# A two-layer attention and retention trunk: bias rows written two rounds later, the output weights' squares started a stage earlier, and the output projection's loads issued in written order

## The chip, the cores and the metric

The kernel runs on one core of a Trainium2 chip. The metric is the device time of one execution in microseconds (us); lower is better. TensorE (PE) multiplies, ScalarE (ACT), VectorE (DVE) and GpSimd (POOL) work on what it produces, and SyncE (SP) issues every DMA of this kernel from one queue, in order.

## The reference

```python
def chunked_rel_attention(q, k, v, rel_bias):      # 8 heads of 64, chunks of 64, own chunk and 8 before
    scores = einsum("bnqhd,bnkhd->bnhqk", qc, kb) * dh ** -0.5
    bias = rel_bias[:, clip(dist, -REL_CLIP, REL_CLIP) + REL_CLIP]
    p = softmax(where(valid, scores + bias, NEG_INF))
    return einsum("bnhqk,bnkhd->bnqhd", p, vb)

def hybrid_layer(x, norm_gain, w_in, w_out, rel_bias, cos, sin):
    proj = rms_norm(x, norm_gain) @ w_in           # x (1, 2048, 1024), w_in (1024, 4096)
    aq, ak, av, ag, rq, rk, rv, rg = split(proj)   # eight sections of 512
    ya = chunked_rel_attention(aq, ak, av, rel_bias)
    yr = chunkwise_retention(rq, rk, rv, cos, sin) # 4 heads of 128, a state from chunk to chunk
    y = concatenate([ya * silu(ag), yr * silu(rg)])
    return x + y @ w_out                           # w_out (1024, 1024)

def reference(x, ...):
    for layer in range(2):
        x = hybrid_layer(x, ...)
    return rms_norm(x, final_gain)
```

## The kernel before

**Split products.** Every large product is float32 made of three float16 products: a tensor is kept as a high and a low half (`hTh`/`hTl`, `whT`/`wlT`, `whV`/`wlV`, `whO`/`wlO`), and a dense tile is 24 matmuls of 128x128 by 128x512 (8 slices of the inner dimension by 3 products), in thirds of 8.

**Stages.** A layer has four groups `s` (two attention heads and one retention head each), and a group four quarters `n` of 512 rows. For each (layer, group, quarter) there are two stages of twelve rounds, a round being 8 matmuls. `dense_T` makes the four feature-major tiles (attention q and k, retention q and k; `dT` in the trace). `dense_V` makes four token-major tiles (values and gates; `dV`). Beside them, a round each time, runs the attention and retention of the quarter *before* (`attention`, `retention`): eight units of three rounds, one for each row tile `a` and head `hx`. A name such as pT1_0_3_0_0 holds layer, group, quarter, row tile and head.

**A unit.** PE makes the scores `S`; DVE adds the bias and takes the maximum (`sc`, L819); ACT takes the exponential (L822) and the high half `pq` (L824); POOL subtracts for the low half (L825); a transposing DMA turns both into `pT` (L827); two units after the scores PE multiplies `pT` by the values (`o`, L835 to L837). Retention multiplies `r` (L869) from `dT` (written by ACT L873 and DVE L877) and the state's halves `sh`. The dense tiles have two PSUM buffers (`psD`): a tile can start when the tile two before it has been read out, for `dense_V` by ACT L775 to L778 and last by DVE L781 to L785 (`gt`).

**Order.** PE, ACT, DVE and POOL execute in the order in which the code is written. `later(k, ...)` puts work k rounds on, `push(generator, steps)` hands background work (weights for the next group) to a list of which `run` takes a share in every round. On SP a list scheduler orders the DMAs, except that those marked by `in_turn` or `keep_in_program_order` may not be moved ahead of what is written before them. A DMA that waits for its buffer holds all DMAs behind it on SP.

**What is touched.** `bias_scratch` writes, at the first quarter of a group, two heads' bias rows 128 times each into HBM (`toep`, L567, 128x767), and `bias_tiles` reads them back skewed (`bias`, L580), masks two corners on POOL and scales on ACT. `prep_Omax` reads `w_out` in eight loads of 512 KB (`stO0m0` to `stO0m7` in layer 0) and squares them on ACT (L312) to find one scale; it is pushed in the second stage of (group 2, quarter 2), and it has the three buffers of the pool `w4`. `prep_O` makes the halves of `w_out`. `wout_first` prepares the first two row tiles of the finished `y` (`yyy`): squares (L963), scale, high rows (L226), low rows (L232); `y_turn` transposes them to `yhy`/`yly`. `wout` is the output projection: sixteen steps of 48 matmuls (`dO`, L1110), six rounds each, with row loads of `y` (`y_load`, L945) and `x` (`x_load`, L954), the sum into `x` (DVE L1113), the store `x_d` (L1119), and in layer 0 the next layer's norm (`residual`: L1006, transposes `ptn` L1011 on PE for some tiles). In its first four steps it runs beside the last attention.

Of the kernel before, what the change touches and what calls it, by code (L numbers as in the profile page):

```python
# [18 lines left out]
P = 128  # L19
# [8 lines left out]
def hybrid_trunk(ctx: ExitStack, tc: tile.TileContext, x, pos, gain, gcol, w_in, w_out, rel, fgain,  # L28
# [468 lines left out]
    def prep_Omax(l, go):  # L497
        nm = f"O{l}"
        mm = b2.tile([P, 1], F32, tag="omax", name=f"omax{nm}")
        st = load_sec(w_out[l, :, 0:P], f"{nm}m0")  # L500
        for j in range(KT):
            yield
            m1 = sumsq(st, f"{nm}m{j}", None)
            if j + 1 < KT:
                st = load_sec(w_out[l, :, (j + 1) * P:(j + 2) * P], f"{nm}m{j + 1}")
            if j == 0:
                dve.tensor_copy(mm, m1)
            else:
# [428 lines left out]
    def y_load(l, t):  # L937
        u = St()
        u.nm = f"y{l}_{t}"
        u.t = t  # L940
        if t < 8:
            u.y = w4.tile([P, D], F32, tag="w4", name=f"yy{u.nm}")
        else:
            u.y = b2.tile([P, D], F32, tag="q", name=f"yy{u.nm}")
        sp.dma_start(u.y, y_d[t])  # L945
        return u

    def x_load(l, u):
# [3 lines left out]
        else:  # L952
            u.x = w4.tile([P, D], F32, tag="w4", name=f"xx{u.nm}")
        sp.dma_start(u.x, x[u.t * P:(u.t + 1) * P, :] if l == 0 else x_d[u.t])  # L954

# [102 lines left out]
    def wout_first(l, go, us):  # L1058
# [4 lines left out]
        for fns in ((), (lambda: y_squares(l, u),), (lambda: y_scale(u, go),), (lambda: rows_hi(u.rows, u.y, u.sy),),  # L1063
                    (lambda: rows_lo(u.rows, u.y, u.sy), lambda: y_squares(l, v)), (lambda: y_turn(u), lambda: y_scale(v, go)),
                    (lambda: rows_hi(v.rows, v.y, v.sy),), (lambda: rows_lo(v.rows, v.y, v.sy),)):
            yield
            for fn in fns:
                fn()
        yield

    def wout(l, go, gc, us, wT=None):
# [6 lines left out]
        for r in range(6 * NT):  # L1078
# [10 lines left out]
            if (i == 1 and T + 1 < NT and (end or T + 2 < NT)) or (i == 5 and hurry):  # L1089
                y_turn(us[T + 1 if i == 1 else T + 2])  # L1090
            if i == 0 and T + 2 < NT:
                us.append(y_load(l, T + 2))
            if i == 1 and T + 1 < NT:
# [282 lines left out]
    for l in range(DEPTH):  # L1376
        gO = [Grp(), Grp()]
        go = Grp()
        for s in range(NSW):
            g = grp(l, s)  # L1380
            for n in range(NS):
# [7 lines left out]
                if n == 0 and not first:  # L1389
                    bs, bt = bias_scratch(l, s), bias_tiles(l, s, g)  # L1390
                    later(1, lambda bs=bs: next(bs))
                    for k in (6, 10, 17, 21):
                        later(k, lambda bt=bt: next(bt))
# [18 lines left out]
                if n == NS - 1 and s == 1 and l + 1 < DEPTH:  # L1412
                    gain_load(l + 1)
                if not first:
                    run(dT, att, 10 if n == 0 else 14 if (l, s, n) == (0, 0, NS - 1) else 22 if (l, s) == (0, 0) else 24)
                if n == NS - 1 and s == NSW - 1:
                    us = []
                    push(wout_first(l, go, us), 10)
                if n == 2 and s == 2:
                    push(prep_Omax(l, go), 13)  # L1420
                if n == NS - 1:
                    if s + 1 < NSW:
                        push(prep_V(l, s + 1, grp(l, s + 1)), 23)
                    else:
                        push(prep_O(l, 1, gO[1], go), 9)
                run(dense_V(l, s, n, g, st), att, 24 if n == NS - 1 and s < NSW - 1 else 12)
# [90 lines left out]
```

## Time and profile before

| | |
|---|---|
| Runs | median of 3: 2081.31 us (2080.66 to 2084.2) |
| Profiled execution | 2082.83 us; its span, first to last instruction, 2081.1 us |
| Mean granted TensorE clock | 0.991 |
| Busy | PE 2006.5 us (96%), DVE 1229.8 (59%), ACT 1139.5 (55%), POOL 683.5 (33%) |
| DMA | 313.63 MB, 65.5% of 16 engines |

Busy time of PE counts pipelined matmuls as covered, so the span less PE's busy time (74.6 us) is what PE stood still. A table of windows gives for stretches of the span their length, each engine's busy time, the mean granted clock (PEclk) and the busy share of the DMA engines: length less PE's busy time is that stretch's standstill, and a clock under 1.00 is time lost at half rate. A row of waits reads: waiting instruction <- releaser: us in total, times, longest. In a timeline a row is start, duration, engine, line, operation, with the idle time before it and its releaser in brackets; SPq rows are the issue of a DMA and not its transfer.

### The profile page before, as it was taken

The numbers are of one execution on the slowest core, as the hardware profiler recorded it, in microseconds if no ns is written. First come the engines' busy times: TensorE is split into PE (matmuls) and PEld (weight loads), VectorE is DVE, ScalarE is ACT, GpSimd is POOL, SyncE is SP. The second block draws the span as 40 slices with busy tenths as digits, with TensorE's granted clock in tenths as the row PEclk, the third lists the DMA queues.
The fourth block names the chain that finished last, engine by engine and source line by source line (L and its number), as shares of the span: only waits on it lengthen the run. The fifth ranks groups of instructions, "written<-read, shape, count | busy, mean of one in ns | idle before, by whom it ended". The sixth has DMA issues, their size and how long they took to land.

```text
span 2081.1 us, 39317 instructions
## 1 busy us (share of the span) xinstructions
PE 2006.5 (96%) x14014; PEld 1052.0 (51%) x14014; DVE 1229.8 (59%) x3817; ACT 1139.5 (55%) x2530; POOL 683.5 (33%) x701
## 2 busy tenths in 40 slices
PE   6988999999999999998999999999999999999998
PEld 4444545555555555544444555555555555554543
DVE  7776556566556555576653556555655565557643
ACT  7566665556565644555443546554655565446432
POOL 0244343444334434430002333444334334343100
PEclk9999999999999999999999999999999999999999
DMA  8678674547484854799765546554755776548874
GB/s 237 162 153 180 142 148 112 114 110 164 117 182 113 167 137 102 153 234 260 203 163 118 125 104 148 120 126 103 152 111 128 178 146 161 127 102 192 211 199 125
DMA packets 645701, 313.63 MB, mean 151 GB/s; under 512 B 459232, under 2 KB 602080, under 8 KB 645504
## 3 DMA queue, kind: packets, MB, share of 16 engines
q1 hardware_dynamic: 645504, 311.12, 65.5%
q8 instruction: 109, 1.79, 0.4%
q14 instruction: 88, 0.72, 0.1%
HBM read 123.26 MB, written 41.98 MB: 79 GB/s over the span
## 4 chain that ended last, share of the span: by engine, by line
PE 49%; DMA 2%; ACT 2%; DVE 1%; issue 0%; SPq 0%; POOL 0%; POOLq 0%; ACTq 0%; DVEq 0%
PE dT L748 15%; PE dV L767 14%; PE dO L1110 13%; PE r L869 2%; DMA pT<-pq 1%; PE S L816 1%; PE S L815 1%; PE o L835 1%; PE o L836 1%; PE o L837 1%; ACT stO1m L312 0%; ACT sc L822 0%; PE ptn L1011 0%; DVE sc L819 0%; ACT pq L824 0%
## 5 line engine op out<-in xcount | busy, mean ns | idle before, releaser
L825 POOL TENSOR_TENSOR pq<-sc,pq 128x640 f16<-128x640 f32 (+4 forms) x256 | 319.6, 1248 | 872.1 <-ACT pq L824 460.2
L822 ACT ACTIVATE sc<-sc,mq,cT 128x640 f32<-128x640 f32 (+4 forms) x256 | 218.4, 853 | 629.4 <-DVE rl L841 338.3
L767 PE MATMUL dV<-whV,hTh 128*128 128x512 f16 x1024 | 353.1, 381 | 4.3 <-DVE gt L785 4.2
L767 PE MATMUL dV<-wlV,hTh 128*128 128x512 f16 x1024 | 353.2, 381 | 0.0
L767 PE MATMUL dV<-whV,hTl 128*128 128x512 f16 x1024 | 353.1, 380 | 0.0
L748 PE MATMUL dT<-hTh,whT 128*128 128x512 f16 x1008 | 349.2, 382 | 2.1 <-DMA hTh<-xa 1.1
L748 PE MATMUL dT<-hTh,wlT 128*128 128x512 f16 x1008 | 348.0, 380 | 0.0
L748 PE MATMUL dT<-hTl,whT 128*128 128x512 f16 x1008 | 347.8, 380 | 0.0
L767 PEld LDWEIGHTS <-hTh 128*128 128x128 f16 x2048 | 196.8, 98 | 219.2 <-DVE gt L785 6.5
L748 PEld LDWEIGHTS <-whT 128*128 128x128 f16 x2016 | 193.0, 98 | 214.9 <-issue 10.6
L819 DVE CUSTOM_DVE_ANT_0 sc<-S,bias 128x640 f32<-128x640 f32 (+4 forms) x256 | 188.3, 736 | 112.7 <-PE S L816 111.3
L1110 PE MATMUL dO<-whO,yly 128*128 128x512 f16 x512 | 194.6, 380 | 1.5 <-DMA yly<-hTl 0.8
L1110 PE MATMUL dO<-whO,yhy 128*128 128x512 f16 x512 | 194.8, 381 | 1.0 <-DMA yhy<-hTh 1.0
L1110 PE MATMUL dO<-wlO,yhy 128*128 128x512 f16 x512 | 194.8, 380 | 0.0
L824 ACT ACTIVATE pq<-sc 128x640 f16<-128x640 f32 (+4 forms) x256 | 171.5, 670 | 8.1
L1110 PEld LDWEIGHTS <-yhy 128*128 128x128 f16 x1024 | 99.9, 98 | 116.1 <-DMA yhy<-hTh 1.5
L767 PEld LDWEIGHTS <-hTl 128*128 128x128 f16 x1024 | 99.3, 98 | 110.6 <-issue 1.9
L748 PEld LDWEIGHTS <-wlT 128*128 128x128 f16 x1008 | 97.5, 98 | 113.1 <-issue 6.2
L815 PE MATMUL S<-k,q 128*128 128x128 f16 (+3 forms) x592 | 142.9, 268 | 0.2
L835 PE MATMUL o<-v,pT 128*128 128x65 f16 x1120 | 130.0, 194 | 12.3 <-DMA pT<-pq 12.3
L836 PE MATMUL o<-v,pT 128*128 128x64 f16 x1120 | 130.2, 195 | 0.0
L816 PE MATMUL S<-k,q 128*128 128x128 f16 (+3 forms) x592 | 130.2, 268 | 0.0
(352 smaller groups left out, 3462.1 us busy)
## 6 DMA issues: line engine op xcount, KB each, us to landing
q<-qq SPq DMA_DIRECT2D x128, 128.0 KB, 2.4
yyy<-y_d SPq DMA_DIRECT2D x32, 512.0 KB, 4.7
stT<-in_w_in_dram SPq DMA_DIRECT2D x27, 512.0 KB, 5.1
stV<-in_w_in_dram SPq DMA_DIRECT2D x26, 512.0 KB, 4.7
k<-kk SPq DMA_DIRECT2D x128, 64.0 KB, 2.0
swp<-rot SPq DMA_DIRECT2D x64, 128.0 KB, 2.7
tabc<-tab SPq DMA_DIRECT2D x32, 256.0 KB, 3.0
tabs<-tab SPq DMA_DIRECT2D x32, 256.0 KB, 3.2
```

The lines of the kernel that those rows point to most:

```text
L748: pe.matmul(ps, w_[:, j, kt, :], h_[:, kt, :], start=(m == 0), stop=(m == 23))
L767: pe.matmul(ps, h_[:, kt, a * P:(a + 1) * P], w_[:, kt, :], start=(m == 0), stop=(m == 23))
L815: pe.matmul(o, st.q[:, hx, 0, cs], k_, start=True, stop=False)
L816: pe.matmul(o, st.q[:, hx, 1, cs], k_, start=False, stop=True)
L819: dve.tensor_tensor_reduce(out=v, in0=S[:, 0:w], in1=g.bias[hx][:, 640 - w:640], scale=1.0, scalar=-3.0e38, op0=ALU.add, op1=ALU.max, accu ...
L822: act.activation(v, v, AF.Exp, bias=m[:, 0:1], scale=g.c[:, 0:1])
L824: act.activation(pq[:, 0:w], v, AF.Copy)
L825: pool.tensor_tensor(pq[:, w:2 * w], v, pq[:, 0:w], op=ALU.subtract)
L835: pe.matmul(o[:, 0:65], u.p[:, b, :], v_[:, 0:65], start=(b == 0), stop=False)
L836: pe.matmul(o[:, 0:64], u.p[:, b, :], v_[:, 65:129], start=False, stop=False)
L869: pe.matmul(out_, w_, m_, start=(i == 0), stop=(i + 1 == len(pairs)))
L1110: pe.matmul(ps, h_[:, kt, :], w_[:, kt, :], start=(m == 0), stop=(m == 23))
```

## The change

Five edits. (1) The writing of the bias rows is put off from one round into the group to three, and reading them back by one round. (2) `prep_Omax` is pushed one stage earlier, spread over 21 steps, and keeps two loads in flight ahead of the squares. (3) `wout_first` is pushed one stage earlier too, `y_turn` of the first tile stands at a fixed round of the last stage, and `prep_O` of the second half has that stage to itself. (4) `y` rows are loaded half a step earlier than before by the code (in round 3 of the step before). (5) `y` loads from row tile 2 on and `x` loads from row tile 1 on are held to the written order on SP.

```diff
     def prep_Omax(l, go):
         nm = f"O{l}"
         mm = b2.tile([P, 1], F32, tag="omax", name=f"omax{nm}")
-        st = load_sec(w_out[l, :, 0:P], f"{nm}m0")
+        load = lambda j: load_sec(w_out[l, :, j * P:(j + 1) * P], f"{nm}m{j}")
+        for _ in range(4):
+            yield
+        sts = [load(0), load(1)]
+        for _ in range(4):
+            yield
         for j in range(KT):
             yield
-            m1 = sumsq(st, f"{nm}m{j}", None)
-            if j + 1 < KT:
-                st = load_sec(w_out[l, :, (j + 1) * P:(j + 2) * P], f"{nm}m{j + 1}")
+            m1 = sumsq(sts[j], f"{nm}m{j}", None)
+            if j + 2 < KT:
+                sts.append(load(j + 2))
@@ y_load
-        sp.dma_start(u.y, y_d[t])
+        i = sp.dma_start(u.y, y_d[t])
+        if t > 1:
+            in_turn(i)
@@ x_load
-        sp.dma_start(u.x, x[u.t * P:(u.t + 1) * P, :] if l == 0 else x_d[u.t])
+        i = sp.dma_start(u.x, x[u.t * P:(u.t + 1) * P, :] if l == 0 else x_d[u.t])
+        if u.t:
+            in_turn(i)
@@ wout_first
-                    (..., lambda: y_squares(l, v)), (lambda: y_turn(u), lambda: y_scale(v, go)),
+                    (..., lambda: y_squares(l, v)), (lambda: y_scale(v, go),),
...
+    def with_turn(gen, us):
+        for r in range(12):
+            if r == 7:
+                y_turn(us[0])
+            next(gen, None)
+            yield
@@ wout
-            if i == 0 and T + 2 < NT:
-                us.append(y_load(l, T + 2))
+            if r == 0 or (i == 3 and T + 3 < NT):
+                us.append(y_load(l, T + 3 if r else 2))
@@ the loop over the stages
-                    later(1, lambda bs=bs: next(bs))
-                    for k in (6, 10, 17, 21):
+                    later(3, lambda bs=bs: next(bs))
+                    for k in (7, 11, 17, 21):
                         later(k, lambda bt=bt: next(bt))
...
+                if n == 2 and s == 2:
+                    push(prep_Omax(l, go), 21)
+                last = n == NS - 1 and s == NSW - 1
+                if last:
+                    us = []
+                    push(wout_first(l, go, us), 9)
                 if not first:
-                    run(dT, att, 10 if n == 0 else ... else 24)
-                if n == NS - 1 and s == NSW - 1:
-                    us = []
-                    push(wout_first(l, go, us), 10)
-                if n == 2 and s == 2:
-                    push(prep_Omax(l, go), 13)
+                    run(dT, att, 12 if last else 10 if n == 0 else ... else 24)
                 if n == NS - 1:
...
-                        push(prep_O(l, 1, gO[1], go), 9)
+                        push(with_turn(prep_O(l, 1, gO[1], go), us), 12)
                 run(dense_V(l, s, n, g, st), att, 24 if n == NS - 1 and s < NSW - 1 else 12)
```

No instruction is added or removed: PE, ACT, DVE, POOL and SP issue the same work in another order. Three places show it.

SP at the start of group 1 of layer 1, before (`stT` is a 512 KB load of the next group's weights, `q1_1_0` the copies of q):

```order
L850 DMA y_d10_115<-ya1_0_2_2_0_16319 128x128
L567 DMA toep1_2_16466<-rel_d_141 128x767
L567 DMA toep1_3_16468<-rel_d_141 128x767
L297 DMA stT1_20_17262<-in_w_in_dram 128x8x128
L827 DMA_TRANSPOSE pT1_0_3_0_0_16499<-pq1_0_3_0_0_16496 128x10x128
L657 DMA q1_1_0_16535<-qq1_1_0_16536 64x1024 x4
```

The same place now:

```order
L855 DMA y_d10_115<-ya1_0_2_2_0_16319 128x128
L297 DMA stT1_20_17262<-in_w_in_dram 128x8x128
L832 DMA_TRANSPOSE pT1_0_3_0_0_16495<-pq1_0_3_0_0_16492 128x10x128
L572 DMA toep1_2_16537<-rel_d_141 128x767
L572 DMA toep1_3_16539<-rel_d_141 128x767
L662 DMA q1_1_0_16531<-qq1_1_0_16532 64x1024 x4
```

The two bias writes have moved from ahead of the transpose to behind it; ten rows on, the read `bias1_2` has moved from ahead of the copies of k to just ahead of the transpose pT1_0_3_1_0. Of the six groups that follow another in a layer, five change in this way. In the first (layer 0, group 1) the scheduler puts the two writes *earlier* than before, between the weight load `stV0_13` and the transpose pT0_0_2_3_1, and not behind a transpose.

ACT where `dense_T` of layer 1, group 2, quarter 2 ends and `dense_V` begins, before:

```order
L824 ACTIVATE pq1_2_1_1_1_21110<-sc1_2_1_1_1_21105 128x640
L917 ACTIVATE state1_2_0_20299<-state1_2_0_20299 128x128
L681 ACTIVATE raw1_2_2_21141<-dT1_2_2_3_21070 128x512
L822 ACTIVATE sc1_2_1_2_0_21191<-sc1_2_1_2_0_21191,mq1_2_1_2_0_21192,cT1_2_17591 128x640
L824 ACTIVATE pq1_2_1_2_0_21196<-sc1_2_1_2_0_21191 128x640
L312 ACTIVATE stO1m0_21206,m1O1m0_21208<-stO1m0_21206 128x1024
```

The same place now:

```order
L829 ACTIVATE pq1_2_1_1_1_21115<-sc1_2_1_1_1_21110 128x640
L312 ACTIVATE stO1m0_20959,m1O1m0_21119<-stO1m0_20959 128x1024
L922 ACTIVATE state1_2_0_20299<-state1_2_0_20299 128x128
L312 ACTIVATE stO1m1_20961,m1O1m1_21142<-stO1m1_20961 128x1024
L686 ACTIVATE raw1_2_2_21156<-dT1_2_2_3_21075 128x512
L312 ACTIVATE stO1m2_21121,m1O1m2_21171<-stO1m2_21121 128x1024
L827 ACTIVATE sc1_2_1_2_0_21211<-sc1_2_1_2_0_21211,mq1_2_1_2_0_21212,cT1_2_17591 128x640
L829 ACTIVATE pq1_2_1_2_0_21216<-sc1_2_1_2_0_21211 128x640
L312 ACTIVATE stO1m3_21144,m1O1m3_21225<-stO1m3_21144 128x1024
```

Three of the eight squares have moved ahead of the unit's exponential; the slot that held square 0 now holds square 3, and so on down, so that the last third of the stage, which held squares 5 to 7, holds none.

SP around the start of layer 0's output projection, before (`yyy0_2` is the load of y row tile 2, `yhy0_1`/`yly0_1` the transposes of tile 1, `hTh1_3`/`hTl1_3` with in_x_dram the loads of x):

```order
L236 DMA_TRANSPOSE yly0_1_12057<-hTh1_2_11663 128x8x128
L827 DMA_TRANSPOSE pT0_3_2_3_0_11858<-pq0_3_2_3_0_11855 128x10x128
L303 DMA stT1_00_1_12894<-in_w_in_dram 128x4x128
L945 DMA yyy0_2_12009<-y_d2_107 128x1024
L235 DMA_TRANSPOSE yhy0_1_12056<-hTh1_2_11663 128x8x128
L928 DMA y_d10_115<-yr0_3_10_11920 128x128
L704 DMA_TRANSPOSE kt0_3_3_11986<-rot0_3_3_3_11569 128x8x128
L303 DMA stT1_00_0_12893<-in_w_in_dram 128x4x128
L945 DMA yyy0_3_12186<-y_d3_108 128x1024
L827 DMA_TRANSPOSE pT0_3_2_3_1_11954<-pq0_3_2_3_1_11951 128x10x128
```

The same place now:

```order
L950 DMA yyy0_2_12009<-y_d2_107 128x1024
L236 DMA_TRANSPOSE yly0_1_12057<-hTh1_2_11334 128x8x128
L961 DMA hTh1_3_11295<-in_x_dram 128x1024
L832 DMA_TRANSPOSE pT0_3_2_3_0_11861<-pq0_3_2_3_0_11858 128x10x128
L235 DMA_TRANSPOSE yhy0_1_12056<-hTh1_2_11334 128x8x128
L303 DMA stT1_00_1_12894<-in_w_in_dram 128x4x128
L933 DMA y_d10_115<-yr0_3_10_11923 128x128
L303 DMA stT1_00_0_12893<-in_w_in_dram 128x4x128
L709 DMA_TRANSPOSE kt0_3_3_11987<-rot0_3_3_3_11604 128x8x128
L855 DMA y_d10_115<-ya0_3_2_2_0_11882 128x128
L832 DMA_TRANSPOSE pT0_3_2_3_1_11957<-pq0_3_2_3_1_11954 128x10x128
```

The load of y tile 3 has gone from ahead of pT0_3_2_3_1 to behind the next transpose, and y tiles 4 and 8 and x tile 2, which were issued before that next transpose, now come one at a time, one y and one x load for each step. In the later steps the x loads of tiles 12 to 14 no longer run ahead either.

More of the change, by code (lines that the diff above doesn't have):

```diff
@@ L1063, in wout_first @@
         for fns in ((), (lambda: y_squares(l, u),), (lambda: y_scale(u, go),), (lambda: rows_hi(u.rows, u.y, u.sy),),
-                    (lambda: rows_lo(u.rows, u.y, u.sy), lambda: y_squares(l, v)), (lambda: y_turn(u), lambda: y_scale(v, go)),
+                    (lambda: rows_lo(u.rows, u.y, u.sy), lambda: y_squares(l, v)), (lambda: y_scale(v, go),),
                     (lambda: rows_hi(v.rows, v.y, v.sy),), (lambda: rows_lo(v.rows, v.y, v.sy),)):
@@ L1413, in hybrid_trunk @@
                     gain_load(l + 1)
-                if not first:
-                    run(dT, att, 10 if n == 0 else 14 if (l, s, n) == (0, 0, NS - 1) else 22 if (l, s) == (0, 0) else 24)
-                if n == NS - 1 and s == NSW - 1:
-                    us = []
-                    push(wout_first(l, go, us), 10)
-                if n == 2 and s == 2:
-                    push(prep_Omax(l, go), 13)
+                if n == 2 and s == 2:
[4 more added lines that the diff above has]
+                    push(wout_first(l, go, us), 9)
+                if not first:
+                    run(dT, att, 12 if last else 10 if n == 0 else 14 if (l, s, n) == (0, 0, NS - 1) else 22 if (l, s) == (0, 0) else 24)
                 if n == NS - 1:
```

## The prediction

> **What bounds the kernel now.** I read the page first: the span, the engines, the chain that ended last.
>
> ```profile
> span 2081.1 us, 39317 instructions
> ...
> PE 2006.5 (96%) x14014; PEld 1052.0 (51%) x14014; DVE 1229.8 (59%) x3817; ACT 1139.5 (55%) x2530; POOL 683.5 (33%) x701
> ```
>
> PE is the bound: it stands still for 2081.1 - 2006.5 = 74.6 us. As the change keeps every instruction, it can gain only standstill, and time at a reduced clock. So the second view is a table of windows over the stages that the edits touch, each cut at the first matmul of its dense tiles.
>
> ```profile
> core 0: us, PE busy (x) PEld busy (x) DVE busy (x) ACT busy (x) POOL busy (x), PEclk, DMA share, GB/s
> 1242.69:1268.84 26.15, 26.15 (x210) 14.47 (x207) 17.17 (x55) 16.48 (x39) 13.48 (x13) 1.00 0.45 92
> 1268.84:1296.53 27.69, 26.28 (x206) 13.97 (x204) 16.43 (x56) 17.38 (x43) 7.00 (x8) 1.00 0.78 181
> 1474.91:1504.76 29.85, 27.97 (x206) 14.38 (x204) 18.08 (x60) 18.70 (x45) 7.00 (x8) 0.94 0.82 174
> 589.30:618.23 28.93, 26.53 (x209) 14.27 (x207) 15.60 (x51) 20.06 (x47) 13.45 (x13) 1.00 0.85 200
> 1604.84:1633.91 29.07, 26.67 (x208) 14.50 (x206) 15.07 (x51) 19.89 (x47) 13.53 (x13) 0.99 0.77 191
> 1633.91:1661.24 27.33, 27.33 (x204) 14.34 (x202) 14.96 (x53) 13.25 (x29) 7.46 (x7) 0.95 0.76 153
> 849.03:877.92 28.89, 26.60 (x207) 14.42 (x205) 18.75 (x56) 18.86 (x40) 15.33 (x13) 1.00 0.61 139
> 877.92:905.00 27.08, 25.00 (x183) 13.06 (x181) 18.14 (x52) 14.60 (x30) 8.18 (x7) 0.94 1.11 255
> 905.00:953.00 48.00, 43.37 (x311) 22.01 (x310) 34.20 (x94) 26.32 (x46) 12.17 (x11) 1.00 1.01 228
> 953.00:1000.00 47.00, 44.52 (x214) 21.71 (x213) 28.07 (x75) 23.79 (x47) 2.20 (x4) 0.96 1.07 255
> 1865.77:1894.66 28.89, 26.59 (x207) 14.40 (x205) 19.05 (x56) 18.96 (x40) 15.62 (x13) 1.00 0.67 129
> 1894.66:1909.71 15.05, 13.39 (x101) 6.75 (x99) 11.40 (x36) 8.66 (x18) 3.36 (x3) 1.00 1.09 294
> 1909.71:2070.00 160.29, 160.29 (x894) 76.88 (x892) 83.28 (x200) 59.48 (x102) 20.11 (x26) 1.00 0.72 183
> ```
>
> The first row is a stage at its best: length and PE busy time are equal, at full clock. Against it, length less busy gives what each touched stage stands: the starts of groups 1 and 2 of layer 1 1.41 and 1.88 us; the stages with the squares 2.40 and 2.40; the last stages 2.29 and 2.30; layer 0's projection 2.08, 4.63 and 2.48; the start of layer 1's 1.66. Four rows have a clock of 0.94 to 0.96; one less it, times the length, is what they lost: 0.06 x 29.85 = 1.8 us, 0.05 x 27.33 = 1.4, 0.06 x 27.08 = 1.6, 0.04 x 47 = 1.9. All this together is 23.5 + 6.7 = 30.2 us: the change can hardly gain more.
>
> **Bias rows (edit 1).** The third view is the waits of PE around the two group starts, then SP's timeline and the chain there, and the landing times of all `pT`.
>
> ```profile
> PE o L835 <- DMA pT<-pq: 3.3, 2, 1.9
> ```
> ```profile
> 1273.85 1.17 SPq L567 DMA_DIRECT2D toep<-rel_d  x2
> ...
> 1275.12 0.53 SPq L297 DMA_DIRECT2D stT<-in_w_in_dram  x1
> ...
> 1276.19 4.97 SPq L827 DMA_TRANSPOSE pT<-pq  x1
> ```
> ```profile
> 1276.19 8.93 DMA pT<-pq
> ...
> 1482.27 9.40 DMA pT<-pq
> ```
> ```profile
> DMA to landing us min/median/max: 2.3/3.0/9.4
> ```
>
> Both stalls (1.41 + 1.88 = 3.29, the 3.3 of the row) are one transpose each, issued right behind the two bias writes and a weight load; it lands after 8.93 and 9.40 us where the median is 3.0. Now it stands ahead of the writes: the 6 us saved exceed the stall, so both go, and with the second its 1.8 of clock: -5.1. What is late next is the bias read, now just ahead of pT1_0_3_1_0; a late transpose there is the unit's own slack, about the median of 3.0, and an issue of 0.53 (a load's row above) fits in it. In layer 0, group 1, the writes now come earlier, ahead of an older transpose: +0 to +1.2 (their 1.17 on SP), I take +0.5, since a transpose usually has slack. Sum -4.6; ends -5.1 and -2.5 (one stall comes back at the next transpose).
>
> **The squares (edit 2).** Waits of PE in the window 589 to 636, the timeline of that stage, and the landing of the loads `stO0m`:
>
> ```profile
> PE r L869 <- ACT dT L873: 1.5, 1, 1.5
> PE r L869 <- DVE dT L877: 0.9, 1, 0.9
> ```
> ```profile
> 595.01 1.04 ACT L312 ACTIVATE stO0m<-stO0m 128x1024 f32<-128x1024 f32 x1
> ...
> 608.29 0.40 DVE L785 SCALAR_TENSOR_TENSOR gt<-gt,dV 128x256 f32<-128x256 f32 x1
> ...
> 608.75 0.39 PE L767 MATMUL dV<-whV,hTh 128*128 128x512 f16 x1
> ```
> ```profile
> DMA to landing us min/median/max: 4.1/4.8/7.3
> ```
>
> PE waits for retention's `dT`, because ACT is late: each square is 1.04 us, in a stage where ACT has 20.06 of 28.93 us. Now squares 0 to 2 stand around the previous stage's end and ahead of unit 2_0's exponential, so ACT is some 1.2 us late there (between one square's 1.04 hidden in part, 0.8, and two, 2.0) and early by as much at the end. The stalls at the end go; but the read-out of the second dense tile ends at 608.29 + 0.40 = 608.69 and PE takes that buffer at 608.75: there is no slack to be late in. So I keep a stall of about 1.55 per layer (1.2 there, 0.35 for the small operations of the squares' sum ahead of `dT`) in place of 2.40: -1.7 in both. Half of the 1.4 of clock behind layer 1's stage goes with it: -0.7. Sum -2.4. Ends: all 4.80 + 1.4 goes, -6.2; two squares late in each stage beside half of the old stall, +2.0.
>
> **The last stages (edit 3).** DVE in that stage, and PE's waits from 870 to 1000:
>
> ```profile
> 867.83 2.04 DVE L336 SCALAR_TENSOR_TENSOR wlO<-stO,o_s,whO 128x1024 f16<-128x1024 f32 x1 [0.51 <-ACT whO L333]
> ...
> 873.91 1.49 DVE L336 SCALAR_TENSOR_TENSOR wlO<-stO,o_s,whO 128x1024 f16<-128x1024 f32 x1 [2.06 <-ACT whO L333]
> ```
> ```profile
> PE o L835 <- DMA pT<-pq: 4.3, 4, 2.1
> PE ptn L1011 <- DVE ymy L966: 2.3, 1, 2.3
> PE r L869 <- DVE sh L877: 1.2, 1, 1.2
> PE r L869 <- DVE dT L877: 1.0, 1, 1.0
> ```
>
> The 2.29 us are the two `r` waits (1.2 + 1.0): DVE is late with `sh` and `dT`, because a low half of `w_out`, 1.5 to 2.0 us, is ahead of each. With `wout_first` a stage earlier the halves spread over twelve rounds and mostly stand behind what PE waits for; one still stands ahead of the last `dT`. I leave 0.6 of 2.3 in each layer (a third of one such row's 2.04): -3.4, ends -4.6 and -1.5. The clock behind it in layer 0: see the next part. The earlier stage takes the rows' squares and transposes; there a transpose now stands behind a 512 KB load on SP: +0 to +1.9 (the worst stall by a late `pT` above), I take +0.3.
>
> **The projection (edits 3 to 5).** Layer 0: of the 4.3 us of late `pT`, 2.1 are one stall in the 877.92 row, behind the `y` loads on SP. That row's clock is 0.94. The changed order puts y tile 3 behind the next transpose: the stall goes, -2.08, and the clock's 1.6 with it. Near 970, `ptn` waits 2.3 us. The timeline tells why, though the row names another releaser:
>
> ```profile
> 963.92 3.34 SPq L236 DMA_TRANSPOSE hTl<-rln  x1
> ...
> 969.75 0.52 SPq L1119 DMA_DIRECT2D x_d<-hTh  x1
> ...
> 973.00 1.28 DVE L1006 SCALAR_TENSOR_TENSOR hTh<-hTh,rsn,gb 128x1024 f32<-128x1024 f32 x1 [5.10 <-DMA x_d<-hTh]
> ```
>
> DVE's norm of an `x` tile overwrites it and waits 5.10 us for its store, which SP issues late, behind transposes (3.34) and loads taken ahead. Held loads come one of each kind a step, so the store goes out earlier: -2.31 with its clock, -1.9. The many small stalls of 905 to 953 (4.63) go with DMA engines at 1.01, which no edit unloads: 0 (ends -4.6 and +2). Layer 1: the 1.66 are the same late `pT`, -1.7; ends -1.7 and -0.8; its later steps stand 0 already. With the clock: -2.08 - 2.31 - 1.9 - 1.7 = -8.0, and -1.6 at 877.92.
>
> **Sum.** -4.6 - 2.4 - (3.4 - 0.3) - 1.6 - 8.0 = -19.7. The profiled execution took 2082.83, so 2063.1. That execution is 1.5 above the median of the runs shown; from the median it is 2061.6.
>
> **The clock, row against rule.** The row with a stall of 1.88 us has 0.94, the one of 877.92 with a single stall of 2.1 has 0.94, the one of 953 with 2.3 has 0.96; those with 1.41 in one stall, and 4.63 in small ones, have 1.00. So here a single stall of about 1.9 us or more costs some 1.7 us of clock, and 6.0 of my 19.7 are this. The Trainium skill, page "TensorE: Matmul & The Clock Gate", section "HAM oscillation — how this bites in real kernels", says that idle gaps of PE over some 3.4 us bring the clock down. By that rule stalls of 2 us would cost no clock, and the reduced clocks would stay where they are or lie elsewhere; the rows speak against it.
>
> **The rivals.**
> *Stalls come back elsewhere.* What goes at one transpose comes back at the next, the squares' lateness all falls on the dense tiles' read-out (+2.0), half of the last stages' stall stays, and the loads help by the two large stalls alone: -2.5 + 2.0 - 2.3 - 4.4 - 0.8 = -8.0, so 2074.8. For it: zero slack at 608.69, and DMA shares over 1.0. Against: the moved transposes are 6 us better off.
> *Everything clears*, the small stalls of 905 to 953 too: -30.1, so 2052.7. Against: DMA at 1.01 to 1.11 there.
> *The clock stays.* Reduced clocks are not bound to the stalls: 19.7 less 6.0 is 13.7, so 2069.1. Speaks for it: 1633.91 has 0.95 without any stall of its own. Against: each of the four comes in or right behind a stage that stands.
> *It doesn't do what it says.* SP's scheduler and the waits give back each stall one for one: about 2081. Against it: five of six group starts change as written.
> *Slower: held loads starve the projection.* An `x` load that no longer runs ahead must wait on SP for its buffer, and holds the transposes behind it. The place is all 16 steps of both layers. A 512 KB load lands 4.1 to 7.3 us after its issue (the row of `stO0m`). It decides from 22.4 / 32 = 0.70 us of stall in each step, where 2063.1 becomes 2085.5. For it: DMA shares over 1.0 in layer 0. Against: layer 1 stands 0 in 160 us at a share of 0.72, with the same loads.
>
> **How the numbers follow.** Forecast 0.52, stalls elsewhere 0.23, everything clears 0.12, clock stays 0.05, one for one 0.04, slower 0.04. The likeliest gives 2063; its own ends are 2056 to 2071. The range of 8 in 10 takes in "everything clears" (2053) and "elsewhere" with 2 us more (2077, where a gain of 0.2% or 4.2 us on the median ends, about what a measurement of this kernel can tell from no change). Beyond it are one for one, slower, and some of the outer cases. Faster by more than 0.2%: 0.52 + 0.23 + 0.12 + 0.05, less 0.02 for "elsewhere" overshooting: 0.90; same 0.06; slower 0.04.
>
> **What the profile after would show.** Bias: the transposes at the starts of groups 1 and 2 of layer 1 land in 3 to 5 us, and the waits for `pT` there are gone; wrong, if a later transpose of the same stage shows them. Squares: the waits for `dT` L873 in the two stages gone, a wait of `dV` for `gt` L785 of about 1.2 new (in the changed kernel these lines stand some five lower); wrong, if the stages are as long as before. Last stages: 2.3 of standstill becomes about 0.6. Projection: the `ptn` wait of 2.3 and the DVE wait of 5.10 for `x_d` gone, PEclk 1.00 in both rows of it. The prediction is wrong if PE standstill falls by less than 7 us, or if it falls as said and the clock does not rise from 0.991.

## The result and the profile after

The changed kernel takes 2065.36 us (median of 4 runs, 2063.26 to 2066.88), beside 2080.98 for the kernel before (4 runs, 2078.07 to 2084.2). The ratio is 0.9924, 95% interval 0.9907 to 0.9941: 15.6 us saved, between 12 and 19. The forecast was 2063. The profiled execution took 2063.26, 19.6 us less than the profiled one of before, so profile against profile hits the forecast sum of 19.7; against the medians that sum is 4 us too large. Part of the agreement of the profiles is chance, as the runs below show.

The head of the page after (span; busy time, share and instructions of each engine):

```profile
span 2061.5 us, 39308 instructions
...
PE 1998.7 (97%) x14014; PEld 1050.5 (51%) x14014; DVE 1231.9 (60%) x3817; ACT 1138.4 (55%) x2530; POOL 686.1 (33%) x701
```

Standstill fell from 74.6 to 62.8 us, by 11.8. The other 7.8 are PE's busy time, which fell from 2006.5 to 1998.7 with the same matmuls, as the mean clock rose from 0.991 to 0.996. The same table of windows as before, of the changed kernel, cut at the same dense tiles (the fourth row is the second stage of group 1 of layer 0, of which the prediction showed none; the third is the stage behind the second group start):

```profile
core 0: us, PE busy (x) PEld busy (x) DVE busy (x) ACT busy (x) POOL busy (x), PEclk, DMA share, GB/s
1257.56:1283.66 26.10, 26.10 (x206) 13.99 (x203) 16.43 (x56) 16.64 (x41) 6.71 (x6) 1.00 0.85 191
1462.04:1488.15 26.11, 26.11 (x206) 14.05 (x204) 16.42 (x56) 16.66 (x42) 6.70 (x6) 1.00 0.85 190
1488.15:1515.96 27.81, 26.09 (x204) 14.15 (x202) 16.88 (x54) 17.16 (x40) 14.91 (x18) 1.00 0.69 135
281.84:308.03 26.19, 26.10 (x204) 14.18 (x202) 16.30 (x54) 16.40 (x38) 14.83 (x17) 1.00 0.70 135
586.92:615.39 28.47, 26.90 (x209) 14.38 (x206) 16.72 (x60) 19.61 (x48) 13.54 (x13) 1.00 1.00 224
1590.12:1618.58 28.46, 26.90 (x209) 14.33 (x207) 18.27 (x60) 19.58 (x48) 13.52 (x13) 1.00 0.96 216
1618.58:1644.66 26.08, 26.08 (x204) 14.03 (x202) 14.56 (x47) 13.14 (x29) 7.46 (x7) 1.00 0.70 133
845.85:872.75 26.90, 26.27 (x207) 14.43 (x205) 18.84 (x46) 15.92 (x35) 15.80 (x13) 1.00 0.79 170
872.75:900.00 27.25, 26.39 (x204) 13.88 (x202) 17.32 (x61) 15.13 (x31) 8.18 (x7) 1.00 0.97 197
900.00:948.00 48.00, 44.35 (x305) 22.73 (x303) 32.09 (x81) 26.15 (x49) 12.72 (x12) 0.96 1.02 237
948.00:995.00 47.00, 46.08 (x230) 22.21 (x228) 33.50 (x84) 27.31 (x51) 2.19 (x4) 1.00 1.01 258
1849.05:1876.60 27.55, 26.26 (x207) 14.43 (x205) 19.34 (x46) 15.98 (x35) 15.71 (x13) 1.00 0.85 157
1876.60:1892.00 15.40, 15.31 (x122) 7.96 (x120) 10.73 (x35) 9.23 (x19) 4.75 (x4) 1.00 0.90 209
```

The reader is to see: the two group starts stand no more (26.10 of 26.10); the stages with the squares still stand 1.57 and 1.56; the last stages 0.63 and 1.29; layer 1's start 0.09. A clock under 1.00 is left in one row, layer 0's projection. New is 1.72 us of standstill in the third row. Waits of PE in layer 0's stage with the squares (586 to 640), with two rows of its timeline, and behind group 2's start (1488 to 1500):

```profile
PE r L874 <- DVE dT L882: 0.8, 2, 0.6
PE dV L772 <- DVE gt L790: 0.6, 1, 0.6
```
```profile
607.35 0.41 DVE L790 SCALAR_TENSOR_TENSOR gt<-gt,dV 128x256 f32<-128x256 f32 x1
...
607.82 0.39 PE L772 MATMUL dV<-whV,hTh 128*128 128x512 f16 x1 [0.64 <-DVE gt L790]
```
```profile
PE o L840 <- DMA pT<-pq: 1.7, 1, 1.7
```

The wait for ACT's `dT` is gone, and the read-out of the dense tile, which had no slack, is the new wait.

### The profile page after: what moved, and what is told of

Same layout as the page of the kernel before. It is cut to its first block, busy times and chain, and to the rows that moved or that the text cites. A ratio compares the mean times of both kernels' runs of the same rounds, so it can differ in the third digit from the quotient of the medians.

```text
span 2061.5 us, 39308 instructions
## 1 busy us (share of the span) xinstructions
PE 1998.7 (97%) x14014; PEld 1050.5 (51%) x14014; DVE 1231.9 (60%) x3817; ACT 1138.4 (55%) x2530; POOL 686.1 (33%) x701
```

## The experiments

Twelve kernels were run beside the changed one, in three groups of four that shared a chip each: the four single edits; rows_loads, u_hold, u_early_y and hold_T; last_late, sq_spread, best and clock_ladder (one run, 2097.36 us, further down). Medians of different groups are of different chips. Ratios are to the kernel before on the same chip; 0.001 is 2.1 us.

| run | what it is | median us | ratio (95%) |
|---|---|---|---|
| changed | all five edits | 2065.36 | 0.9924 (0.9907 to 0.9941) |
| e_bias | edit 1 alone | 2076.55 | 0.9977 (0.9963 to 0.9991) |
| e_squares | edit 2 alone | 2077.11 | 0.9986 (0.9974 to 0.9999) |
| e_rows | edit 3 alone | 2078.13 | 0.9981 (0.9969 to 0.9993) |
| e_loads | edits 4 and 5 | 2077.69 | 0.9981 (0.9969 to 0.9992) |
| rows_loads | edits 3, 4, 5 | 2067.58 | 0.9946 (0.9933 to 0.9959) |
| u_hold | changed without 5 | 2071.22 | 0.9959 (0.9947 to 0.9970) |
| u_early_y | changed without 4 | 2065.32 | 0.9936 (0.9923 to 0.9948) |
| hold_T | changed, weight loads held too | 2062.44 | 0.9919 (0.9906 to 0.9932) |
| last_late | hold_T, halves later | 2063.47 | 0.9918 (0.9905 to 0.9931) |
| sq_spread | hold_T, squares spread | 2063.40 | 0.9917 (0.9903 to 0.9930) |
| best | sq_spread, halves later | 2064.48 | 0.9923 (0.9910 to 0.9936) |

The runs tell single edits from nothing, not from each other. What tells them apart is the standstill of a stage in the profiles (us; T is dense_T, V dense_V, s/q group and quarter):

| run | 0: V 1/0 | 0: V 2/2 | 0: V 3/3 | 0: proj. | 1: T 1/0 | 1: T 2/0 | 1: V 2/0 | 1: V 2/2 | 1: V 3/3 | 1: proj. |
|---|---|---|---|---|---|---|---|---|---|---|
| before | 2.03 | 2.40 | 2.29 | 9.19 | 1.41 | 1.88 | 0 | 2.40 | 2.30 | 1.66 |
| e_bias | 0 | 2.70 | 2.29 | 9.77 | 0 | 0 | 0 | 2.40 | 2.29 | 2.03 |
| e_squares | 0.11 | 1.47 | 2.29 | 9.87 | 1.08 | 1.92 | 0.80 | 2.66 | 2.30 | 0 |
| e_rows | 0.60 | 2.41 | 0.59 | 10.27 | 1.64 | 0.45 | 1.50 | 2.41 | 1.61 | 2.29 |
| e_loads | 0.59 | 2.41 | 2.29 | 8.12 | 1.42 | 0.88 | 0.03 | 2.41 | 2.30 | 3.21 |
| rows_loads | 0.91 | 2.57 | 0.58 | 5.82 | 1.03 | 0 | 0.28 | 2.40 | 1.54 | 0.89 |
| u_hold | 0 | 1.44 | 1.10 | 10.15 | 0 | 0 | 0.26 | 1.67 | 1.61 | 2.10 |
| u_early_y | 0.11 | 1.52 | 1.44 | 8.30 | 0 | 0 | 0 | 1.45 | 1.88 | 0 |
| changed | 0.09 | 1.57 | 0.63 | 5.43 | 0 | 0 | 1.72 | 1.56 | 1.29 | 0.09 |
| clock_ladder | 0.32 | 1.45 | 2.20 | 6.88 | 0 | 0 | 0 | 2.74 | 1.60 | - |
| hold_T | 0 | 1.69 | 0.89 | 6.55 | 0 | 0 | 0 | 1.38 | 1.22 | 0 |

Up to layer 1's projection clock_ladder has the changed kernel's instructions in the same order on every engine, so its row is a second execution of the changed kernel (its last column would hold stalls that were added). Two stages come out quite differently in it, layer 1's with the squares and layer 0's last one:

```profile
1586.21:1615.86 29.65, 26.91 (x210) 14.36 (x207) 16.87 (x60) 19.84 (x48) 13.51 (x13) 1.00 0.96 210
841.94:870.75 28.81, 26.61 (x207) 14.25 (x205) 18.66 (x46) 15.96 (x35) 15.70 (x13) 1.00 0.78 171
```

They stand 2.74 and 2.20 us, where the changed kernel's own profile has 1.56 and 0.63 and the kernel before 2.40 and 2.29. So a difference of 1 to 2 us in one stage of one profile may be chance.

**Each edit alone.** e_bias is this and no more:

```diff
-                    later(1, lambda bs=bs: next(bs))
-                    for k in (6, 10, 17, 21):
+                    later(3, lambda bs=bs: next(bs))
+                    for k in (7, 11, 17, 21):
```

> The kernel before with edit 1 alone (bias rows written in round 3, read back in rounds 7 and 11). My theory: the two transposes at the starts of groups 1 and 2 of layer 1 land in 3 to 5 us instead of 8.9 and 9.4, both stalls (1.41 and 1.88 us) go and with the second one window of half clock (1.7 us): -3.5 to -5 us. Rival, stalls come back one transpose later: -1 to +1 us, with a new stall of 1.4 to 2 us at the unit 1_1 of one of these groups. On the start of group 1 of layer 0 (2.03 us of standstill before, none after, which I had not forecast): if edit 1 removes it, it is gone here too; if it is chance in how two weight loads land, it may stand here as before, and the untouched stages of the other runs show it now and then.

Measured 4.3 us less. Both stalls are gone, here and in every kernel with edit 1; of the five without it all keep the first (1.03 to 1.64), and the second is there in all but one. The transposes, which landed 8.93 and 9.40 us after their issue, land after 3.40 and 4.00 in e_bias and after 3.28 and 4.11 in the changed kernel, and no later one of the stage is waited for. So the moved transposes are the cause. The start of group 1 of layer 0 is another matter. These are its windows in the kernels before, e_squares and e_loads, the last two without edit 1:

```profile
280.51:310.31 29.80, 27.77 (x204) 14.70 (x202) 17.25 (x54) 16.97 (x40) 15.04 (x16) 0.94 0.70 122
```
```profile
282.21:308.42 26.21, 26.10 (x205) 14.15 (x202) 17.11 (x54) 16.90 (x40) 14.74 (x16) 1.00 0.72 135
```
```profile
281.77:308.45 26.68, 26.09 (x204) 14.17 (x202) 17.16 (x54) 16.86 (x40) 15.06 (x16) 1.00 0.72 136
```

The 2.03 us and the half clock behind them are gone without the edit: the profile of before showed a bad case of a stall whose length varies from execution to execution. The 1.72 us that the changed kernel has at V 2/0 is of the same kind (0 to 1.50 elsewhere, with edit 1 and without).

e_squares moves the push and the loads of `prep_Omax` as the change does:

```diff
+                if n == 2 and s == 2:
+                    push(prep_Omax(l, go), 21)
                 if not first:
                     run(dT, att, ...)
-                if n == 2 and s == 2:
-                    push(prep_Omax(l, go), 13)
```

> The kernel before with edit 2 alone (squares of the output weights across two stages). My theory: each of the two stages with the squares goes from 28.9 to 29.1 us down to 28.4 to 28.5, the wait for ACT's half of dT is replaced by a wait of the dense tile for the read-out gt of about 0.6 us, and layer 1's window of half clock behind that stage goes or stays by chance of 1.7 us: -1 to -3 us in all. Rival, the squares' lateness only moves: within 0.5 us of before.

3.7 us less by the medians, 0.2 to 5.4 by the interval. Layer 0's stage does what was expected (28.93 to 28.38 us). Layer 1's, at 29.42 us, doesn't: beside the same 0.64 and 0.58 it waits 1.44 for a small DVE operation of the scale's sum. The same wait makes the 2.74 of clock_ladder; what brings it on in two executions of seven is not known. In the other stages of the kernels with these squares the gain is about half a microsecond. Besides, a half clock stands at the end of the stage with the squares, or right behind it, in five of the ten such stages of kernels without edit 2, and in none of the eighteen with it.

e_rows is the change's `wout_first` and `with_turn` without the rest, e_loads its `y_load` and `x_load`:

```diff
-                    push(wout_first(l, go, us), 10)
+                    push(wout_first(l, go, us), 9)
...
-                        push(prep_O(l, 1, gO[1], go), 9)
+                        push(with_turn(prep_O(l, 1, gO[1], go), us), 12)
```
```diff
-        sp.dma_start(u.y, y_d[t])
+        i = sp.dma_start(u.y, y_d[t])
+        if t > 1:
+            in_turn(i)
...
-            if i == 0 and T + 2 < NT:
-                us.append(y_load(l, T + 2))
+            if r == 0 or (i == 3 and T + 3 < NT):
+                us.append(y_load(l, T + 3 if r else 2))
```

> The kernel before with edit 3 alone (first finished rows a stage earlier). My theory: the last stage of each layer goes from 28.9 us to about 26.9 to 27.6 (-2.0 and -1.3), the half clock behind layer 0's goes (-1.6), layer 1's stall behind it goes in part (-0.5): -4 to -6 us. Rival: without the held loads, the y and x loads that the scheduler takes ahead now start earlier and put the transposes of the last stage behind them, which gives back 2 us or more: -2 to 0.

> The kernel before with edits 4 and 5 alone (y loaded half a step earlier by the code, y and x loads held to written order). My theory: the stall of 2.3 us at the layer norm's transposes near 972 goes with its window of half clock (-4.0), the late transpose behind the y loads of the projection's start goes in part (-1 to -2), layer 1's start gains 0.5 to 1.5: -5 to -8 us. Rival, held loads arrive late: stalls for y, x or their transposes of 0.5 us or more per step, 0 to +5 us.

2.7 and 3.1 us less by the medians, 4.0 each by the ratios: less than the theories' 4 to 6 and 5 to 8 by the medians, at their lower edge or below it by the ratios. The last stages gained about as expected in e_rows (0.59 and 1.61 us of standstill are left), and the layer norm's wait near 970 shrank from 2.31 to 0.33 us in e_loads. But layer 1's projection became worse in both. This is SP there, first e_rows, then e_loads, then the changed kernel:

```profile
1881.42 0.53 SPq L945 DMA_DIRECT2D yyy<-y_d  x1
1882.06 2.09 SPq L827 DMA_TRANSPOSE pT<-pq  x1
...
1887.41 1.81 SPq L945 DMA_DIRECT2D yyy<-y_d  x2
```
```profile
1878.47 1.03 SPq L297 DMA_DIRECT2D stO<-in_w_out_dram  x2
1879.59 4.83 SPq L236 DMA_TRANSPOSE yly<-hTh  x1
1884.47 0.57 SPq L956 DMA_DIRECT2D hTh<-x_d  x1
1885.14 1.32 SPq L827 DMA_TRANSPOSE pT<-pq  x1
```
```profile
1872.10 1.50 SPq L961 DMA_DIRECT2D hTh<-x_d  x1
1873.70 1.66 SPq L832 DMA_TRANSPOSE pT<-pq  x1
```

With the rows alone, free `y` loads stand around the transpose, which lands 7.97 us after its issue; with the loads alone, the first tile's `yly` transposes still share SP with the loads of `w_out`, one is 4.83 us in issue, and the attention's transpose goes out 3.3 us after its input was ready. With both it is issued behind one `x` load and lands after 4.83. So the two edits should need each other there, which the next kernel asked.

**What needs what.** rows_loads joins the two diffs above.

> The kernel before with edits 3, 4 and 5 (rows earlier and loads held). My theory, from the windows of the single edits: alone, rows changed the two projections by -2.0 and +2.1 us and the loads by -4.5 and +3.2, while the changed kernel has -5.8 and -1.5, so the two edits need each other: with the last stages' -2.0 and -1.2 here about -8 to -11 us. Rival, they only add: -1.2 in the projections and -3.3 in the last stages, -4 to -6 us.

11.7 us less; the ratio, 0.54% (0.41 to 0.67), is 11.2 us, where the two alone sum to 0.38%, 7.9 us, with intervals of 2.5 us each. The waits of PE for `pT` at layer 1's projection (e_rows, e_loads, rows_loads, u_hold):

```profile
PE o L835 <- DMA pT<-pq: 2.3, 1, 2.3
```
```profile
PE o L835 <- DMA pT<-pq: 3.2, 2, 2.9
```
```profile
PE o L835 <- DMA pT<-pq: 0.9, 1, 0.9
```
```profile
PE o L840 <- DMA pT<-pq: 2.1, 2, 1.9
```

In the changed kernel the wait is not there at all. The eight profiles with both edits stand 0 to 0.9 us there (clock_ladder ahead of its first added stall); of the six that lack one or both, five stand 1.7 to 3.2. The sixth, e_squares, has neither edit and stands 0, so the place can also come out well by chance. The length of the projections from their first matmul, with the clock in it, points the same way. Layer 1's takes 186.0 to 186.8 us in the three profiles with none of edits 3 to 5, 188.5 with the rows alone and in u_hold, 189.6 with the loads alone, 186.5 in u_early_y and 184.4 to 185.4 in the others with both: there each alone loses and the two together gain. Layer 0's takes 195.7 to 197.3, 194.7 with the rows alone, 192.3 with the loads alone, 190.2 in rows_loads: there they only add. In the runs as a whole nothing more than adding shows either: the four single edits sum to 0.75%, and the change has 0.76%.

u_hold takes the two `in_turn` out of the changed kernel, u_early_y puts `y_load` back to the first round of a step:

```diff
-        i = sp.dma_start(u.y, y_d[t])
-        if t > 1:
-            in_turn(i)
+        sp.dma_start(u.y, y_d[t])
```
```diff
-            if r == 0 or (i == 3 and T + 3 < NT):
-                us.append(y_load(l, T + 3 if r else 2))
+            if i == 0 and T + 2 < NT:
+                us.append(y_load(l, T + 2))
```

> The changed kernel without edit 5 (y and x loads not held on SP). If holding the loads is what frees the transposes at the projections' starts: slower than the changed kernel by 3 to 7 us (2068 to 2072), with stalls for late pT at layer 1's projection start of 1.5 us or more and the wait at the layer norm's transposes of layer 0 back. Rival, the earlier y load (edit 4) does it: within 1.5 us of the changed kernel.

> The changed kernel without edit 4 (y rows loaded in the first round of a step, as before, but held to written order). If the earlier place matters only because the loads are held: y arrives late for the norm and its transposes, stalls in the projections, +1 to +4 us over the changed kernel. Rival, six rounds of lead are enough either way: within 1 us.

Without the holding 5.9 us are lost by the medians, 7 by the ratios, and layer 0's projection stands 10.15 instead of 5.43 us. The layer norm's wait is back; u_hold and, beside it, e_loads:

```profile
PE ptn L1016 <- DVE ymy L971: 1.9, 1, 1.9
```
```profile
PE ptn L1015 <- DVE ymy L970: 0.3, 1, 0.3
```

It is 1.9 to 2.3 us in all five profiles without held loads and at most 0.6 in all nine with them, so holding the loads is its cure. Without the early `y` nothing is lost that can be told from noise: the medians are the same, the ratios 2.5 us apart with intervals that overlap. The one profile of u_early_y is of its slowest run (2071.58, the others 2063.64 to 2067.03) and its layer 0 projection stands 8.30 us, where the others with edits 3 to 5 have 5.43 to 7.12. Whether edit 4 is worth anything stays open.

**Weight loads held too.** The stall of varying length (layer 0's V 1/0, layer 1's V 2/0) has two 512 KB loads ahead of its transpose on SP, which the scheduler takes from the next stage (SP in the changed kernel):

```profile
1487.77 2.38 SPq L297 DMA_DIRECT2D stT<-in_w_in_dram  x2
1491.89 3.51 SPq L832 DMA_TRANSPOSE pT<-pq  x1
```
```diff
-            sp.dma_start(st, v)
+            (in_turn if nm[0] == "T" else keep)(sp.dma_start(st, v))
```

> The changed kernel, and in addition the 512 KB loads of the next group's dense_T weights held to written order on SP, so that the two loads ahead of the transpose of unit 1_1 in each group's second stage move into the stage after. My theory: the standstill there (1.72 us in group 2 of layer 1 of the changed kernel's profile, 0 to 2.03 in other profiles, and the 0.1 to 0.6 of others) goes in all six groups, -1 to -3 us: 2062 to 2064. Rival, the loads then arrive too late for their squares and ACT falls behind, or the transposes of another unit stand behind them: 0 to +4 us.

In the five groups that have such loads the transpose lands 2.9 to 3.9 us after its issue, where the changed kernel's took 3.6 to 6.2, and the slack that PE finds is 0.5 to 1.4 instead of 0.05 to 0.7. The stalls there are 0 in hold_T and in the three kernels built on it; group 3 of layer 1, which has no such loads ahead, stood 1.08 in hold_T. The median is 2062.4, 2.9 below the changed kernel, but on another chip; by the ratios it is 1 us, well inside the intervals. The mechanism is shown, the gain isn't.

**Squares spread, halves later.** sq_spread starts the squares four rounds earlier and rests a round after each second one; last_late moves the last work on `w_out`'s halves:

```diff
-        for _ in range(4):
+        for _ in range(2):
             yield
         sts = [load(0), load(1)]
-        for _ in range(4):
+        for _ in range(2):
             yield
...
+            if j % 2:
+                yield
             m1 = sumsq(sts[j], f"{nm}m{j}", None)
```
```diff
-            next(gen, None)
+            for _ in range((1, 1, 1, 1, 1, 1, 1, 1, 1, 1, 0, 2)[r]):
+                next(gen, None)
```

> The kernel hold_T with the squares of the output weights started four rounds earlier and one idle round after each second square. If the stalls that the change left in those two stages (1.57 and 1.56 us, read-out of the dense tile and dT) come from ACT and DVE being late by squares in successive rounds: both stages fall from 28.5 to 26.1 to 27 us, -2 to -4 us against hold_T (2058 to 2060). Rival, the squares are then late beside other tight places in the stage before: within 1 us of hold_T or slower.

> The kernel hold_T with the work on the output weights' halves that stands in the last stage's eleventh round put into its twelfth, behind retention's dT. If the low half ahead of dT on DVE makes the stalls that the change left in the last stages (0.63 and 1.29 us): both go, -1 to -2 us. Rival, the low half is then ahead of the next unit's scores, its transpose is late and PE waits at the start of the projection: 0 to +3 us.

> The kernel hold_T with both of the edits of sq_spread and last_late. If both are independent, the sum of what they do: 2057 to 2061.

sq_spread: the rival. The read-out wait is gone, and a wait of 1.2 to 1.3 us for `dT` is there in its place in both layers; the stages take 28.21 and 29.52 us (layer 1's waits 1.4 for `pT` besides), the time is as hold_T's. last_late tested nothing: `prep_O` has nine steps, so the tenth round and later hold none of it, and not one instruction changed its place. It is a second sample of hold_T (and best of sq_spread, at 2064.48 and not the 2057 to 2061 of a sum): same order, and standstill in the last stages of 1.24 and 1.54 against 0.89 and 1.22. What the low half ahead of `dT` on DVE costs was therefore not tried.

**The clock.** clock_ladder adds, to the changed kernel, twelve stalls to layer 1's projection:

```diff
+                if end and c == 0 and 3 <= t < 15:
+                    n = (0, 300, 500, 600, 700, 800, 900, 1000, 1100, 1300, 1600, 2000)[t - 3]
+                    for o in range(0, n, D):
+                        xd = u.x[:, 0:min(D, n - o)]
+                        keep(dve.scalar_tensor_tensor(out=xd, in0=xd, scalar=1.0, in1=xd, op0=ALU.mult, op1=ALU.max))
+                    keep(dve.tensor_copy(u.h[:, 0, :], u.h[:, 0, :]))
```

> The changed kernel with twelve stalls of PE put into layer 1's output projection, where it otherwise doesn't stand: in each of the row tiles 3 to 14 DVE works longer on the row and then rewrites the first weights of the next half with their own values, so that PE waits about 1 us for the first and up to 3 to 4 us for the last, some 11 us apart. From the profiles so far I hold that the clock is judged on a fixed grid of 3.41 us, and that a stretch of the grid in which PE idles over about 1.9 us is followed by one at half clock: then the low stretches here follow exactly those grid stretches with over 2.05 us idle, none with under 1.8, and a stall of 2 to 2.8 us that a boundary of the grid cuts in two even parts costs no clock. Rival one, the length of a single stall decides (over 1.9): every rung over 1.9 us is followed by a low stretch wherever the grid lies. Rival two, only gaps over 3.4 us bring the clock down: at most the last rung or two.

Low stretches in the profiles begin a whole number of 3.413 us apart. Windows cut on that grid, each with the stretch behind it (length less PE busy is what PE idled in it):

```profile
1971.63:1975.04 3.41, 1.54 (x9) 0.71 (x9) 3.26 (x8) 0.00 (x0) 0.00 (x0) 1.00 0.70 270
1975.04:1978.46 3.42, 3.42 (x17) 1.55 (x16) 0.26 (x3) 1.15 (x1) 0.00 (x0) 1.00 0.40 158
1995.52:1998.94 3.42, 1.34 (x7) 0.49 (x6) 2.31 (x4) 0.00 (x0) 0.00 (x0) 1.00 0.94 324
1998.94:2002.35 3.41, 3.41 (x10) 1.24 (x9) 1.42 (x6) 1.15 (x1) 0.00 (x0) 0.50 0.40 159
2009.18:2012.59 3.41, 1.68 (x8) 0.58 (x6) 1.66 (x2) 0.00 (x0) 0.00 (x0) 1.00 1.16 239
2012.59:2016.00 3.41, 2.96 (x14) 1.38 (x15) 2.18 (x8) 1.15 (x1) 0.00 (x0) 1.00 0.63 247
2036.48:2039.90 3.42, 1.80 (x9) 0.60 (x7) 1.55 (x2) 0.00 (x0) 0.00 (x0) 1.00 1.03 263
2039.90:2043.31 3.41, 2.34 (x11) 1.09 (x12) 2.76 (x9) 0.67 (x1) 0.00 (x0) 1.00 0.39 159
2043.31:2046.72 3.41, 3.41 (x17) 1.56 (x16) 0.36 (x1) 0.47 (x1) 0.00 (x0) 1.00 0.27 109
```

A stall of 2.08 us inside one stretch (1995.52) is followed by 0.50. One of 1.87 (1971.63) isn't. Those of 2.19 and 2.69 us, cut by a boundary into 1.73 + 0.45 and 1.62 + 1.07, cost no clock; the other three over 2.4 us (2.48, 3.00 and 3.42) each left 2.05 us or more in one stretch and were followed by 0.50. Both rivals fall: neither the length of a single stall nor gaps over 3.4 us decide.

## Why the prediction was right, and where it wasn't

**Bound and sign.** PE is the bound, the gain was standstill and clock, and it came from the places named. "Slower" and "one for one" did not happen, nor "stalls come back elsewhere" as a whole.

**Bias rows, -4.6.** The two starts gave 1.59 and 3.74 us, 5.3 with the clock, as worked out (5.1). The +0.5 for the earlier writes in layer 0 was nothing. What the prediction left out is how much the landing of a transpose behind two weight loads varies from execution to execution (3.7 to 6.2 us after its issue at layer 0's V 1/0, over the ten profiles that have those loads ahead): 3.6 us of the difference of the two profiles lie there and are none of the change's, and 1.9 were lost at layer 1's V 2/0 (25.92 us before, 27.81 now) likewise.

**Squares, -2.4.** Measured -0.46, -0.61 and -1.25 of clock: -2.3. The stall of 1.55 per layer is 1.57 and 1.56, but made otherwise: 0.64 at the read-out, not 1.2, and about 0.9 at `dT` and in small gaps, not 0.35. That the size came out is partly luck: clock_ladder has 2.74 in layer 1.

**Last stages, -3.4.** 28.89 to 26.90 and 28.89 to 27.55, -3.3. Layer 0 kept the 0.6 forecast, layer 1 1.29. Over the ten profiles with edit 3 layer 0 keeps 0.57 to 2.20 and layer 1 1.16 to 1.88, so 0.6 was too little for layer 1, and in layer 0 this profile is near the best. The +0.3 for the transposes was nothing: the stage before stands 0 (26.08 of 26.08).

**Projections, -8.0 and -1.6 of clock.** Measured -5.8 and -1.5 with the clock, 2.3 too little. The stall near 970 went as said, by holding the loads (e_loads, u_hold), and DVE's wait for `x_d` ahead of it fell from 5.10 to 1.05. The stall of 2.08 at the start is 0.86 now, but another of 2.08 stands at 915 with its half clock: the term took the small stalls of 905 to 953 as fixed, and one of them has grown (in clock_ladder no wait for `pT` there is over 1.1). Layer 1's 1.66 did go. But the prediction gave these gains to the held loads, and with them alone layer 1's start stands 3.21 in e_loads: there it takes the earlier rows too.

**Sum.** In the two profiles the terms gave 5.3 + 2.3 + 3.3 + 7.3 = 18.2 us, not 19.7. That the profiles still differ by 19.6 is luck: the stalls of varying length, 3.6 less 1.9, fill the gap.

**Clock, row against rule.** The rows were right in that stalls of some 2 us, far under 3.4, can cost 1.7 us of clock, and the half clocks fell from five to one behind the first 200 us. They were read as a matter of the single stall's length, though, and one of them was put down to the wrong stall. These are stretches of the grid in the kernel before:

```profile
875.29:878.71 3.42, 1.48 (x13) 0.91 (x14) 3.38 (x13) 1.94 (x6) 0.55 (x1) 1.00 1.22 248
878.71:882.12 3.41, 3.41 (x23) 1.73 (x21) 1.62 (x4) 3.38 (x7) 1.40 (x1) 0.50 1.07 260
...
885.53:888.95 3.42, 2.27 (x11) 0.83 (x9) 2.78 (x7) 3.16 (x8) 1.37 (x1) 1.00 1.12 308
888.95:892.36 3.41, 2.48 (x26) 1.47 (x27) 2.10 (x9) 0.26 (x3) 0.57 (x2) 1.00 1.07 373
```

The half clock of the 877.92 row begins at 878.71, nine microseconds ahead of the late `pT` that the prediction charged it to. It follows the two stalls of about 1 us at the end of the last stage, which edit 3 shortens and which fall into one stretch with 1.94 us idle. The late `pT` of 2.08 us itself (887.80 to 889.88) is cut by a boundary into 1.15 + 0.93 and cost no clock. So the grid decides, and part of the 6 us is where it happens to lie. The spread of the runs goes with the clock too: of 35 runs of the kernel before on one chip, the eight at a mean clock of 0.992 have a median of 2083.6 us and the seven at 0.995 one of 2077.8. How much of that is the grid's place and how much the stalls themselves is not shown.

## What to carry to other kernels

Where one queue issues all DMAs, look at what stands just ahead of each transfer that an engine waits for: letting the `y` and `x` loads run ahead again cost 5.9 us by the medians and 7 by the ratios here. Try edits to one queue together as well as alone: two that each lost at layer 1's projection gained there together. Before a stall in one profile is put into a sum, or its absence into a gain, look at another profile of the same code.

## What the runs showed of the hardware that was not expected

The clock is judged on a grid of 3.413 us that runs on through the execution. Over the 14 profiles, leaving out the first 30 us (the record of the clock begins only 15 to 26 us in), stretches that were already at half clock and the end of the kernel, none of 216 stretches in which PE idled 1.0 to 1.83 us was followed by one at half clock, 53 of 53 with 2.06 us or more were, and 11 of the 22 between. One at half clock costs 1.7 us. The Trainium skill, page "TensorE: Matmul & The Clock Gate", section "What's actually happening", gives a free-running window of 4096 cycles, 3413 ns, which the grid agrees with; its idle window of about 3.4 us does not agree with 2.06. The end of the kernel, where PE has no work left, goes the same way (the changed kernel):

```profile
2054.00:2057.41 3.41, 0.26 (x2) 0.00 (x0) 1.51 (x3) 1.32 (x3) 0.55 (x1) 1.00 0.38 154
2057.41:2060.82 3.41, 0.00 (x0) 0.00 (x0) 0.15 (x1) 0.12 (x1) 0.00 (x0) 0.50 0.39 154
```

In all 14 profiles the first such stretch with 2.14 us or more idle is followed by half clock, and the five before it with 0.20 to 1.44 are not. What decides between 1.84 and 2.05 us stays open.

A stretch at half clock can be followed by another with less idle time: behind the first 30 us all eleven that were at 0.50 and had 0.94 to 1.62 us idle were followed by one at 0.50, where a stretch at full clock needed 1.84 or more; one with 0.73 was not.
